# Strassen's algorithm for both products of the MLP, with the first half begun in the out product

## The chip, the cores and the metric

One Trainium2 chip, one core. The metric is the device time of one launch in microseconds, as the median of the runs. Times of single operations come from one profiled execution.

The engines of a core run their own instruction streams in order and wait for one another by semaphores: TensorE (PE in the profile) multiplies, with weight loads (PEld) of their own; VectorE (DVE), ScalarE (ACT) and GpSimd (POOL) do the rest; SyncE (SP) issues the DMA transfers.

## The reference

One decoder layer over 1024 tokens of 1024 features: an attention branch and a time-mixing branch (RWKV-7), their gated merge and out product, and then the MLP, which most of the change concerns:

```python
mix_out = merged @ w_out[l]
x = (x + gt1 * rms_norm(mix_out, norm_mix_post[l])).astype(x.dtype)

h = rms_norm(x, norm_ffn_pre[l]) * (1.0 + sc2) + sh2
f = jnp.square(jax.nn.relu(h @ w_ff1[l])) @ w_ff2[l]      # 1024 -> 4096 -> 1024
x = (x + gt2 * rms_norm(f, norm_ffn_post[l])).astype(x.dtype)
```

The time mixing is computed for pairs of heads and in 16 chunks of tokens: for each head and chunk a Gram product, 64 features of the head deep, is formed first.

## The kernel before

The stages follow one another: attention (to about 500 us), time mixing (to about 1300), merge (to about 1480), out product (to about 1576), MLP (to the end).

**Exact products.** Every large product is computed in three fp32r matmuls: each operand is split into a high part and a remainder, and hi*hi, hi*lo and lo*hi are summed. `split` (L62 to L66) makes them: ScalarE casts the high part (L65), and VectorE or, where it is named, GpSimd subtracts it from the whole (L66). A matmul has 128 contracted rows, 128 columns of weights and 512 moving columns.

**MLP.** The 4096 hidden features are 32 tiles of 128. `ff1` makes two tiles at a time: 8 contracted blocks x 3 products x 2 halves of the tokens, 48 matmuls of L308 per tile, 1536 in all; ScalarE squares the ReLU, and the tile is split at once and stays in SBUF. `ff2` adds the product of the two feature tiles with their rows of `w_ff2` to the result of all 8 token tiles (1536 matmuls of L1162; VectorE adds each PSUM tile to the sum, L1168). Weights come as 128 KB loads `w_t` (L293, two staging tiles) and 512 KB loads `w2t` (L1126) on SyncE's queue; their splits run on ScalarE and VectorE. GpSimd only scales in the last block (L1139).

**Out product and the join.** `out_product` goes over token tiles: product (L984), norm and residual, then `transposed` turns the normed tile into feature rows (TensorE L1043), scales them on VectorE (L1052, L1053) and ScalarE (L1048) and splits them into `hh`, `hl`. Before the tokens 512 to 1023 are through, `ff1_head` starts the first two feature tiles with the first half of the tokens (L308).

**Gram products.** `pair_gram` (L734) has for each of 4 blocks and each of 2 heads one PSUM tile of 4 products (L750), which VectorE then masks into two tiles (L754, L756). The two heads' features lie in partitions 0 to 63 and 64 to 127. `attend` (L494) forms the attention's scores, also 64 deep, head by head in turn (L503).

**Order.** A scheduler orders each engine's stream when the program is built, by the code's order and by when tiles come free; tiles of one name share a ring of buffers, so that a new tile waits for the last use of an old one.

Of the kernel before, what the change touches and what calls it, by code (L numbers as in the profile page):

```python
# [29 lines left out]
NP2 = 6  # L30
NPS = 0
# [19 lines left out]
class Block:  # L51
# [682 lines left out]
    def pair_gram(self, st, pr, m):  # L734
# [229 lines left out]
    def out_product(self, cst, big, w1, psD, psS, xS):  # L964
# [3 lines left out]
        with ExitStack() as es:  # L968
# [66 lines left out]
            def transposed(group, xs):  # L1035

                hh, hl = hhs[group[0] // 4], hls[group[0] // 4]
                for n, i in enumerate(group):
                    x, tl = xs[n], slice(128 * (i % 4), 128 * (i % 4) + 128)
                    for b in range(2):  # L1040
# [4 lines left out]
                        ht = t2.tile([128, 4, 128], F32, name="ht")  # L1045
# [11 lines left out]
            for group in OGR:  # L1057
                todo.append((group, residual(group)))
                if len(todo) > 1:
                    transposed(*todo.pop(0))  # L1060
            self.hh2, self.hl2 = [[[t[:, k, :] for k in range(KT)] for t in ts_] for ts_ in (hhs, hls)]
            self.ff1_head(w1, psD)
            transposed(*todo[0])

    def load_w1(self, w1, j):
        return self.load_w(w1, self.w("w_ff1")[:, 128 * j:128 * j + 128], "w", 2, 8, 2)

    def ff1_head(self, w1, psD):
# [27 lines left out]
    def mlp(self, cst, big, w1, psD, psS, xS):  # L1096
        nc, tc = self.nc, self.tc
        FB = 2
        with ExitStack() as es:
            pool = lambda n, b, **kw: self.pool(es, n, b, **kw)  # L1100
            yp, w2, fp, sm = pool("yp", 1), pool("w2", 2 * FB), pool("fp", 2 * FB), pool("sm3", 4)
            g2 = yp.tile([128, D], F32, name="g2")
            nc.sync.dma_start(g2, self.row_bc(self.rS[1][0]))
            yb = [big.tile([128, 4, D], F32, name="big") for i in range(2)]
            y = [yb[i // 4][:, i % 4, :] for i in range(NT)]
            nb = DFF // 128 // FB

# [131 lines left out]
```

## Time and profile before

| | us |
|---|---|
| time before, median of 3 runs (2299.31 to 2305.64) | 2300.22 |
| the profiled execution, its own time | 2297.36 |
| its span | 2295.6 |
| TensorE busy | 2151.7 |
| VectorE busy | 1365.4 |
| ScalarE busy | 943.3 |
| GpSimd busy | 392.9 |
| last matmul of the MLP ends | 2285.07 |

The rows of the trace are in a section of their own below. A window row gives a stretch, its length, and the busy time of each engine in it (with the number of instructions), then the granted TensorE clock as a share of full speed. A row of the chain of waits gives the start, the duration and the engine, tile and line of one piece of the chain that ended last. A timeline row joins instructions of a group that follow one another and, in brackets, the idle time before them. Two matmul records belong to one fp32 product, as L503 and L750 are, and one to an fp32r product, as L308, L984 and L1162 are; some records can be missing.

### The profile page before, as it was taken

To read this page: it belongs to the slowest core of one execution; us is meant where nothing else is said; L and a number is where in the kernel's file an instruction comes from. 1 tells how busy PE (TensorE), PEld (TensorE's weight loads), DVE (VectorE), ACT (ScalarE), POOL (GpSimd) and SP (SyncE) were. 2 spreads that over 40 slices of the span, in tenths; PEclk is the share of its full clock that TensorE was granted. 3 is DMA by queue.
4 is the path that set the end of the run, shared out by engine and by line. 5 is a ranking of instruction groups with operands and counts; after the bars stand their busy time and mean duration, and the time that the engine had idled before them with its cause. 6 is when DMAs were issued, how large, how long until landed. Compare 5 with 4: busy or idle time off the path is not lost. (4 is left out here: it accounts for less than half of the span.)

```text
span 2295.6 us, 28645 instructions
## 1 busy us (share of the span) xinstructions
PE 2151.7 (94%) x10410; PEld 1705.6 (74%) x10410; DVE 1365.4 (59%) x2638; ACT 943.3 (41%) x1868; POOL 392.9 (17%) x388
## 2 busy tenths in 40 slices
PE   6898999988998989898999999998999999999998
PEld 3676676766776767777777778876888888888887
DVE  5845555467979788777978634338434434434435
ACT  5544534345455546445554442227422222232222
POOL 2504310321313222221313123201000000000002
PEclk9899999998999999989998999999999999999999
DMA  7513311100111010101011264413221111111113
GB/s 252 171 31 102 101 35 38 54 26 21 31 31 36 29 36 24 47 19 42 27 33 49 69 203 148 142 51 114 82 60 40 49 58 42 46 58 44 37 42 147
DMA packets 151212, 152.96 MB, mean 67 GB/s; under 512 B 10618, under 2 KB 118292, under 8 KB 151072
## 3 DMA queue, kind: packets, MB, share of 16 engines
q1 hardware_dynamic: 151071, 151.14, 20.7%
q8 instruction: 82, 1.34, 0.2%
q14 instruction: 59, 0.48, 0.1%
HBM read 129.07 MB, written 22.03 MB: 66 GB/s over the span
## 5 line engine op out<-in xcount | busy, mean ns | idle before, releaser
L65 ACT CAST w_h<-w_t 128x256 fp32r<-128x256 f32 x368 | 147.8, 404 | 480.2 <-PE d L308 366.6
L308 PE MATMUL d<-hh,w_h 128*128 128x512 f32 x960 | 327.7, 413 | 8.2 <-ACT w_h L65 4.7
L308 PE MATMUL d<-hl,w_h 128*128 128x512 f32 x960 | 331.9, 416 | 2.9 <-DVE hl L281 2.9
L308 PE MATMUL d<-hh,w_l 128*128 128x512 f32 x960 | 324.5, 410 | 0.1
L308 PE MATMUL d<-big,w_h 128*128 128x512 f32 (+1 forms) x1056 | 281.1, 385 | 1.9 <-ACT big L65 1.4
L66 POOL TENSOR_TENSOR w_l<-w_t,w_h 128x256 fp32r<-128x256 f32 x160 | 128.3, 803 | 634.9 <-ACT w_h L65 288.4
L308 PEld LDWEIGHTS d<-big,w_h 128*128 128x128 f32 x1056 | 197.9, 190 | 41.5 <-ACT big L65 1.8
L308 PEld LDWEIGHTS d<-hh,w_h 128*128 128x128 f32 x960 | 181.1, 193 | 46.7 <-ACT w_h L65 5.5
L1168 DVE TENSOR_TENSOR big<-big,d 128x1024 f32<-128x1024 f32 (+1 forms) x113 | 136.8, 1211 | 132.3 <-PE d L1162 132.2
L308 PEld LDWEIGHTS d<-hl,w_h 128*128 128x128 f32 x960 | 180.9, 192 | 45.0 <-issue 9.8
L308 PEld LDWEIGHTS d<-hh,w_l 128*128 128x128 f32 x960 | 181.0, 192 | 42.3 <-issue 8.6
L66 DVE TENSOR_TENSOR w_l<-w_t,w_h 128x256 fp32r<-128x256 f32 x208 | 102.0, 492 | 168.0 <-ACT w_h L65 102.1
L308 PE MATMUL d<-big,w_l 128*128 128x512 f32 (+1 forms) x528 | 163.9, 384 | 0.0
L1162 PE MATMUL d<-w2l,fh 128*128 128x512 f32 x512 | 158.3, 389 | 0.0
L1162 PE MATMUL d<-w2h,fl 128*128 128x512 f32 x512 | 158.3, 389 | 0.0
L1162 PE MATMUL d<-w2h,fh 128*128 128x512 f32 x512 | 158.3, 389 | 0.0
L65 ACT CAST w2h<-w2t 128x1024 fp32r<-128x1024 f32 x32 | 33.7, 1052 | 270.2 <-PE d L1162 238.7
L1139 POOL TENSOR_TENSOR big<-big,g 128x1024 f32<-128x1024 f32 x6 | 14.4, 2396 | 670.8 <-DVE big L1168 670.8
L154 POOL TENSOR_TENSOR macc<-macc,ada_t 128x512 f32<-128x512 f32 x56 | 87.8, 1571 | 177.6 <-ACT macc L152 158.9
L308 PEld LDWEIGHTS d<-big,w_l 128*128 128x128 f32 x528 | 100.1, 190 | 19.3
L1162 PEld LDWEIGHTS d<-w2h,fl 128*128 128x128 f32 x512 | 96.1, 188 | 20.0
L1162 PEld LDWEIGHTS d<-w2h,fh 128*128 128x128 f32 x512 | 96.1, 188 | 19.9
(337 smaller groups left out, 3788.1 us busy)
## 6 DMA issues: line engine op xcount, KB each, us to landing
w_t<-in_w_in_dram SPq DMA_DIRECT2D x240, 128.0 KB
ada_t<-in_ada_w_dram SPq DMA_DIRECT2D x64, 256.0 KB
w_t<-in_w_ff_dram SPq DMA_DIRECT2D x128, 128.0 KB
w2t<-in_w_ff_dram SPq DMA_DIRECT2D x32, 512.0 KB
x<-in_x_dram SPq DMA_DIRECT2D x16, 512.0 KB
ada_t<-in_ada_w_dram SPq DMA_DIRECT2D x16, 512.0 KB
gS<-gt SPq DMA_DIRECT2D x32, 256.0 KB
wbr_t<-in_w_branch_dram SPq DMA_DIRECT2D x16, 320.0 KB
```

Of the source, the lines that this page charges most:

```text
L65: nc.scalar.copy(hi, t)
L66: (eng or nc.vector).tensor_tensor(lo, t, hi.bitcast(F32), OP.subtract)
L154: nc.gpsimd.tensor_tensor(acc, acc, t, OP.add)
L308: nc.tensor.matmul(p[:, 512 * half + cs.start:512 * half + cs.stop], a, b[half][k][:, cs], start=k == ks[0] and i == 0, stop=k == ks[-1] a ...
L1139: (nc.vector if i >= NP2 else nc.gpsimd).tensor_tensor(z[i][:, cs], y[i][:, cs], g2[:, cs], OP.mult)
L1162: nc.tensor.matmul(p[:, cs], a[:, ts_], w[:, cs], start=e == 0 and n == 0, stop=e == len(r) - 1 and n == 2)
L1168: nc.vector.tensor_tensor(y[i][:, cs], y[i][:, cs], p[:, cs], OP.add)
```

## The change

**Strassen.** A product of 2 x 2 blocks takes 7 block products in place of 8 in the form of Winograd. Both MLP products use it, each as a phase of its own, so that the features go to DRAM (`fS`) between them.

- `ff1`: 16 pairs of feature tiles (256 features). Blocks of features x contracted halves x token halves; a block product is 12 matmuls, a pair 84 in place of 96. The operands on the tokens' side (T1 to T4, B22) are made once, those on the weights' side (S1 to S4) per pair, all split by ScalarE and VectorE.
- `ff1_head`: for the first 8 pairs the products P1 and P2, which need only the first half of the tokens, run in the out product, 24 matmuls per pair, two pairs ahead of the last transposition and six behind it. P1 goes to DRAM (`uS`); P1 + P2 is the first feature block.
- `ff2`: 8 chunks of 512 features. Seven go by Strassen: 168 matmuls in place of 192; a block product is 24 matmuls into 2 x 2 PSUM banks, and VectorE gathers it into five sums (11, U, 22, 21, 12) of 4 x 512 columns a partition. Splits and sums of the features run on VectorE (`va`), those of the weights on GpSimd (`vb`). The last chunk is plain, by token rows, each followed by norm and output.
- `transposed` for tokens 512 to 1023 keeps the rows whole (`h1`) and makes T2 = B22 - (B12 - B11).
- `pair_gram` takes both heads' PSUM tiles at once and goes over products before heads.

The diff, cut to its core:

```diff
@@ pair_gram
         for b in range(4):
-            for h in range(2):
-                hp = slice(64 * h, 64 * h + 64)
-                p = psS.tile([128, 4, 128], F32, name="s")
-                for c in range(4):
-                    cc = 4 * b + c
-                    nc.tensor.matmul(p[:, c, :].rearrange("p (a t) -> p a t", t=32),
+            ps = [psS.tile([128, 4, 128], F32, name="s") for h in range(2)]
+            for c in range(4):
+                cc = 4 * b + c
+                for h in range(2):
+                    hp = slice(64 * h, 64 * h + 64)
+                    nc.tensor.matmul(ps[h][:, c, :].rearrange("p (a t) -> p a t", t=32),
                                      bk[hp, cc].rearrange("p a t -> p (a t)"), ar4[hp, :, cc, :],
                                      start=True, stop=True)
+            for h in range(2):
+                p = ps[h]
@@ out_product, transposed
-                        self.split(ht, hh[:, 4 * b:4 * b + 4, tl], hl[:, 4 * b:4 * b + 4, tl])
+                        if i < 4:
+                            self.split(ht, self.hh0[:, 4 * b:4 * b + 4, tl], self.hl0[:, 4 * b:4 * b + 4, tl])
+                    if i >= 4:
+                        t = t2.tile([128, 4, 128], F32, name="ht")
+                        nc.vector.tensor_tensor(t, self.h1[:, 0:4, tl], self.hh0[:, 0:4, tl].bitcast(F32), OP.subtract)
+                        nc.vector.tensor_tensor(t, t, self.hl0[:, 0:4, tl].bitcast(F32), OP.subtract)
+                        nc.vector.tensor_tensor(t, self.h1[:, 4:8, tl], t, OP.subtract)
+                        self.split(t, self.T2[:, 0, :, tl], self.T2[:, 1, :, tl])
...
-            self.ff1_head(w1, psD)
+            self.ff1_head(w1, ut, ft, psD, range(2))
             transposed(*todo[0])
+            self.ff1_head(w1, ut, ft, psD, range(2, NH))
+    def ff1_head(self, w1, ut, ft, psD, gs):
...
+            for n, (g, p) in enumerate(pair):
+                self.quarter(p, ws[0][n], hs(range(4)), True)
+                u = ut.tile([128, 512], F32, name="u")
+                self.nc.scalar.copy(u, p)
+                self.nc.sync.dma_start(self.uS[g], u)
+            for n, (g, p) in enumerate(pair):
+                self.quarter(p, ws[1][n], hs(range(4, 8)), False)
+                self.feature(ft, p, 2 * g, 0)
+    def feature(self, ft, p, j, half):
+        t = ft.tile([128, 512], F32, name="ft")
+        nc.scalar.activation(t, p, AF.Relu)
+        nc.scalar.activation(t, t, AF.Square)
+        nc.sync.dma_start(self.fS[j // 4][:, j % 4, 512 * half:512 * half + 512], t)
+    def quarter(self, p, a, b, start):
+        for k, ((ah, al), (bh, bl)) in enumerate(zip(a, b)):
+            for i, (s, m) in enumerate(((ah, bh), (ah, bl), (al, bh))):
+                self.nc.tensor.matmul(p, s, m, start=start and k == 0 and i == 0, stop=k == len(a) - 1 and i == 2,
+                                      skip_group_check=not start)
+    def ff1(self, big, big2, opn, tmp, ut, ft, ps):
...
+        with self.tc.high_priority():
+            for q in range(2):
...
+                nc.vector.tensor_tensor(t, h1[:, k2], h1[:, ks], OP.subtract)
+                self.split(t, T3[:, 0, ks], T3[:, 1, ks])
...
+        def weights(g):
+            raw = tmp.tile([128, KT, 256], F32, name="t8")
+            nc.sync.dma_start(raw, src[:, :, 256 * g:256 * g + 256])
...
+            sums = tmp.tile([128, 4, 4, 128], F32, name="t8")
...
+            nc.vector.tensor_tensor(S1, A[2, 1], A[2, 2], OP.add)
...
+                o = opn.tile([128, 2, 4, 128], F32R, name="op")
+                self.split(t, o[:, 0], o[:, 1])
...
+            run("P6", x[:, 1], True)
+            nc.vector.tensor_tensor(u, u, x[:, 1], OP.add)
...
+            run("P7", y[:, 0], True)
+            v = ut.tile([128, 512], F32, name="u")
+            nc.vector.tensor_tensor(v, u, y[:, 0], OP.add)
+            run("P5", y[:, 1], True)
+            nc.vector.tensor_tensor(v, v, y[:, 1], OP.add)
+            self.feature(ft, v, 2 * g + 1, 1)
...
+    def ff2(self, big, big2, opn, tmp, ut, sm, ps, xS):
...
+            (va, vb), f = (nc.vector, nc.gpsimd), {}
+            ops = {"P1": (operand(fr[:, k1, h1], va), operand(wr[:, k1, h1], vb))}
+            va.tensor_tensor(sa[:, 0], fr[:, k1, h2], fr[:, k2, h2], OP.add)
+            va.tensor_tensor(sa[:, 1], sa[:, 0], fr[:, k1, h1], OP.subtract)
+            vb.tensor_tensor(sb[:, 0], wr[:, k1, h2], wr[:, k1, h1], OP.subtract)
+            vb.tensor_tensor(sb[:, 1], wr[:, k2, h2], sb[:, 0], OP.subtract)
...
+                        nc.vector.tensor_tensor(acc[nm][h], acc[nm][h], ps2[h], OP.add)
...
+            product("P1", x, True)
+            gather("U", x, True)
+            ops["P6"] = operand(sa[:, 1], va), operand(sb[:, 1], vb)
```

The pools of the MLP are `opn` with 12 operand tiles of 4 KB a partition, `tmp` with two tiles of each name (`t8`, `t4`), and PSUM as four tiles of two banks (`m`).

TensorE in the first pair of heads, at the first Gram group: `s` is the PSUM tile of a head and a block, `ar` and `b8` the operands. Before:

```order
L750 MATMUL s_4023<-ar_3972,b8_3973 128x128 x4
L750 MATMUL s_4030<-ar_3972,b8_3973 128x128 x4
L308 MATMUL d_4226<-hh_437,w_l_4217 128x512 x2
L308 MATMUL d_4226<-hh_437,w_h_4222 128x512 x2
L308 MATMUL d_4226<-hl_438,w_h_4222 128x512 x2
L308 MATMUL d_4226<-hh_437,w_l_4223 128x512 x2
L308 MATMUL d_4226<-hh_437,w_h_4222 128x512 x2
L308 MATMUL d_4226<-hl_438,w_h_4222 128x512 x2
L308 MATMUL d_4226<-hh_437,w_l_4223 128x512 x2
L308 MATMUL d_4302<-hh_437,w_h_4280 128x512
L750 MATMUL s_4037<-ar_3972,b8_3973 128x128 x4
L750 MATMUL s_4044<-ar_3972,b8_3973 128x128 x4
```

After:

```order
L749 MATMUL s_4039<-ar_3988,b8_3989 128x128
L749 MATMUL s_4040<-ar_3988,b8_3989 128x128
L749 MATMUL s_4039<-ar_3988,b8_3989 128x128
L749 MATMUL s_4040<-ar_3988,b8_3989 128x128
L749 MATMUL s_4039<-ar_3988,b8_3989 128x128
L749 MATMUL s_4040<-ar_3988,b8_3989 128x128
L749 MATMUL s_4039<-ar_3988,b8_3989 128x128
L749 MATMUL s_4040<-ar_3988,b8_3989 128x128
L307 MATMUL d_4242<-hh_453,w_l_4233 128x512 x2
```

Eight products in two runs of four have become eight in turn; this is the first of the pair's four groups. At the second group the row after is x3, x3, x1, x1, at the third and fourth x4, x4 as before.

VectorE at the join, from the last token tiles on: `ht` is a transposed tile, `w_l` the remainder of a weight tile. Before:

```order
L1052 TENSOR_TENSOR ht<-s,m_574 128x512
L1053 TENSOR_TENSOR ht<-ht,m_574 128x512
L66 TENSOR_TENSOR w2l<-w2t,w2h 128x1024
L66 TENSOR_TENSOR big<-ht,big 128x4x128 x2
L66 TENSOR_TENSOR w_l<-w_t,w_h 128x256 x2
L66 TENSOR_TENSOR w2l<-w2t,w2h 128x1024
L66 TENSOR_TENSOR w_l<-w_t,w_h 128x256
L66 TENSOR_TENSOR fl<-ft,fh 128x1024
L66 TENSOR_TENSOR w_l<-w_t,w_h 128x256
L66 TENSOR_TENSOR fl<-ft,fh 128x1024
L66 TENSOR_TENSOR w_l<-w_t,w_h 128x256
```

After, where `t` and `big` of 128x1024 are the tokens' operands:

```order
L1061 TENSOR_TENSOR ht<-big,ht 128x512
L65 TENSOR_TENSOR big<-ht,big 128x4x128
L65 TENSOR_TENSOR w_l<-w_t,w_h 128x256
L1147 TENSOR_TENSOR t_13418<-big 128x1024
L1147 TENSOR_TENSOR t_13422<-big 128x1024
L65 TENSOR_TENSOR w_l<-w_t,w_h 128x256
L65 TENSOR_TENSOR big<-t_13418,big 128x1024
L65 TENSOR_TENSOR big<-big 128x1024
L65 TENSOR_TENSOR big<-t_13422,big 128x1024
L1152 TENSOR_TENSOR t_13426<-big 128x1024
L1152 TENSOR_TENSOR t_13436<-big 128x1024
L1153 TENSOR_TENSOR t_13426<-t_13426,big 128x1024
```

Ten more rows of `big` and `t` follow before the next `w_l`; 16 instructions of 128x1024 stand between these two weight splits.

VectorE in the steady state of ff2, one block before (`fl`, `w2l`: remainders of features and weights; `big<-big,d`: the sum from PSUM):

```order
L1168 TENSOR_TENSOR big<-big,d 128x1024
L66 TENSOR_TENSOR fl<-ft,fh 128x1024
L1168 TENSOR_TENSOR big<-big,d 128x1024 x6
L66 TENSOR_TENSOR w2l<-w2t,w2h 128x1024
L1168 TENSOR_TENSOR big<-big,d 128x1024
L66 TENSOR_TENSOR w_l<-w_t,w_h 128x256
L66 TENSOR_TENSOR w2l<-w2t,w2h 128x1024
L66 TENSOR_TENSOR w_l<-w_t,w_h 128x256 x3
L66 TENSOR_TENSOR fl<-ft,fh 128x1024
L66 TENSOR_TENSOR w_l<-w_t,w_h 128x256 x4
```

and part of a chunk after (`op`: an operand's remainder; `big<-big,m`: the sums from PSUM; `t`: sums of operands):

```order
L65 TENSOR_TENSOR op<-big,op 128x1024
L1282 TENSOR_TENSOR big<-big,m 128x1024
L1264 TENSOR_TENSOR t_15945<-big 128x1024
L1265 TENSOR_TENSOR t_15945<-t_15945,big 128x1024
L1282 TENSOR_TENSOR big<-big,m 128x1024
L65 TENSOR_TENSOR op<-t_15681,op 128x1024
L1282 TENSOR_TENSOR big<-big,m 128x1024 x2
L65 TENSOR_TENSOR op<-big,op 128x1024
L1282 TENSOR_TENSOR big<-big,m 128x1024 x2
L65 TENSOR_TENSOR op<-t_15945,op 128x1024
L1295 TENSOR_TENSOR t_15945<-big,t_15945 128x1024
L1282 TENSOR_TENSOR big<-big,m 128x1024 x2
```

GpSimd has no instruction there before; after, one chunk is:

```order
L1266 TENSOR_TENSOR t_16474<-big 128x1024
L1267 TENSOR_TENSOR t_16474<-big,t_16474 128x1024
L65 TENSOR_TENSOR op<-big,op 128x1024
L65 TENSOR_TENSOR op<-t_16474,op 128x1024
L1296 TENSOR_TENSOR t_16474<-big,t_16474 128x1024
L65 TENSOR_TENSOR op<-big,op 128x1024
L65 TENSOR_TENSOR op<-t_16588,op 128x1024
L1299 TENSOR_TENSOR t_16852<-big 128x1024
L65 TENSOR_TENSOR op<-t_16474,op 128x1024 x2
L65 TENSOR_TENSOR op<-big,op 128x1024
```

VectorE's splits stand each between two pairs of sums from PSUM, and GpSimd's eleven instructions are new.

## Rows read from the trace of the kernel before

**Rows 1.** The page: busy time by engine, granted clock in 40 slices, chain by line.
```profile
PE 2151.7 (94%) x10410; PEld 1705.6 (74%) x10410; DVE 1365.4 (59%) x2638; ACT 943.3 (41%) x1868; POOL 392.9 (17%) x388
...
PEclk9899999998999999989998999999999999999999
...
PE d L1162 15%; PE d L308 15%; DVE big L66 0%; DVE junk L1024 0%; DVE x L1026 0%; ACT junk L1029 0%; DVE ht L1052 0%; ACT x L1032 0%; ACT junk L1015 0%; PE s L1043 0%; ACT ht L1048 0%; DVE big L1147 0%; DVE my L1013 0%; DVE ht L1053 0%; DVE rn_t L1092 0%
```

**Rows 2.** Chain of waits, 1700 to 1800: start us, us, what.
```profile
1700.24 21.76 PE d L308 x96
1722.00 21.76 PE d L1162 x96
```

**Rows 3.** Windows by stage: stretch, its us, busy us of each engine, clock, DMA.
```profile
core 0: us, PE busy (x) PEld busy (x) DVE busy (x) ACT busy (x) POOL busy (x), PEclk, DMA share, GB/s
500.00:600.00 100.00, 90.13 (x489) 72.19 (x488) 83.17 (x187) 49.51 (x104) 19.16 (x25) 0.93 0.08 22
1590.00:1600.00 10.00, 6.50 (x54) 6.12 (x52) 6.94 (x20) 7.04 (x20) 1.57 (x1) 0.97 0.57 191
1600.00:1610.00 10.00, 7.17 (x31) 6.50 (x32) 5.79 (x9) 6.61 (x12) 0.00 (x0) 0.51 0.27 86
1700.00:1800.00 100.00, 100.00 (x443) 82.81 (x442) 40.64 (x47) 26.37 (x39) 0.00 (x0) 1.00 0.19 57
```

**Rows 4.** Chain of waits, 1570 to 1606 and beyond: the join.
```profile
1577.27 5.08 PE d L308 x21
...
1601.23 1.10 PE s L1043 x4
1602.36 0.70 DVE ht L1052
...
1603.69 1.22 DVE w2l L66
1604.91 0.61 DVE big L66
1605.57 29.39 PE d L308 x142
```

**Rows 5.** Chain of waits, 2230 to the end.
```profile
2285.07 0.69 DVE big L1168
...
2286.79 1.29 DVE big L1147
...
2291.65 0.66 DVEq L1235
```

**Rows 6.** Timeline of TensorE, a Gram group: start, us, line, out<-in, records.
```profile
484.42 1.71 PE L750 MATMUL s<-ar,b 64*128 64x128 f32 x16 [2.49 <-DVE ar L710]
486.06 0.73 PE L308 MATMUL d<-hh,w_l 128*128 128x512 f32 x2
```

**Rows 7.** Timeline of TensorE in the attention, scores of one and of two heads.
```profile
128.04 0.70 PE L503 MATMUL s<-k,q 64*128 64x256 f32 x2
128.67 0.44 PE L522 MATMUL s<-ident,pr 128*128 128x128 f32 x2
...
129.40 0.70 PE L503 MATMUL s<-k,q 64*128 64x256 f32 x4
130.03 1.09 PE L534 MATMUL po<-pts,vt 128*64 128x128 f32 x14
```

**Rows 8.** Timeline of VectorE in the merge.
```profile
1380.80 1.22 DVE L942 SCALAR_TENSOR_TENSOR gr<-gr,d 128x1024 f32<-128x1024 f32 x1 [5.67 <-PE d L308]
1381.94 0.82 DVE L66 TENSOR_TENSOR wbr_l<-wbr_t,wbr_h 128x640 fp32r<-128x640 f32 x1
...
1387.91 2.47 DVE L66 TENSOR_TENSOR wbr_l<-wbr_t,wbr_h 128x640 fp32r<-128x640 f32 x1 [0.47 <-ACT wbr_h L65]
```

**Rows 9.** Timeline of SyncE's queue after the join.
```profile
1604.94 0.33 SPq L1126 DMA_DIRECT2D w2t<-in_w_ff_dram  x1
...
1626.56 15.19 SPq L293 DMA_DIRECT2D w_t<-in_w_ff_dram  x9
```

**Rows 10.** Groups by line on VectorE, 1600 to the end: busy, mean ns, idle before.
```profile
L1168 DVE TENSOR_TENSOR big<-big,d 128x512 f32<-128x512 f32 x2 | 1.4, 685 | 0.1
```

**Rows 11.** Groups by line on GpSimd, 1640 to the end.
```profile
L1139 POOL TENSOR_TENSOR big<-big,g 128x1024 f32<-128x1024 f32 x6 | 14.4, 2396 | 670.8 <-DVE big L1168 670.8
```

**Rows 12.** Timeline of GpSimd in the merge.
```profile
1386.84 2.86 POOL L66 TENSOR_TENSOR big<-wos,big 128x1024 fp32r<-128x1024 f32 x1 [1.68 <-ACT big L65]
1394.98 2.40 POOL L66 TENSOR_TENSOR big<-wos,big 128x1024 fp32r<-128x1024 f32 x1 [5.28 <-ACT big L65]
```

**Rows 13.** Timeline of VectorE in the time mixing.
```profile
691.25 0.41 DVE L756 TENSOR_TENSOR fe<-s,gmask 128x256 f32<-128x256 f32 x1
691.58 0.42 DVE L754 TENSOR_TENSOR b<-s,gmask 128x256 f32<-128x256 f32 x1
691.91 0.41 DVE L756 TENSOR_TENSOR fe<-s,gmask 128x256 f32<-128x256 f32 x1
```

**Rows 14.** Timeline of GpSimd in the time mixing.
```profile
691.31 1.29 POOL L728 TENSOR_TENSOR rkv<-rkv 128x512 f32<-128x512 f32 x1
```

**Rows 15.** Waits of SyncE's queue, 1600 to 1900: sum, times, longest.
```profile
SPq L1126 <- DMA w2t<-in_w_ff_dram: 11.1, 8, 4.4
```

More of the change, by code (lines that the diff above doesn't have):

```diff
@@ L29 @@
 DFF = 4096
-NP2 = 6
-NPS = 0
+NH, NU, NF, NOP = 8, 4, 3, 12
 OGR = ((0, 1), (2, 3), (4,), (5,), (6,), (7,))
@@ L1044, in transposed @@
                                                 self.ident)
-                        ht = t2.tile([128, 4, 128], F32, name="ht")
+                        ht = t2.tile([128, 4, 128], F32, name="ht") if i < 4 else self.h1[:, 4 * b:4 * b + 4, tl]
                         if b:
@@ L1053, in transposed @@
                             nc.vector.tensor_tensor(ht, ht, bc(sh), OP.add)
-                        self.split(ht, hh[:, 4 * b:4 * b + 4, tl], hl[:, 4 * b:4 * b + 4, tl])
+                        if i < 4:
[6 more added lines that the diff above has]
+                        self.split(t, self.T2[:, 0, :, tl], self.T2[:, 1, :, tl])
             todo = []
             for group in OGR:
+                if group[0] == 0:
+                    self.hh0, self.hl0 = [big.tile([128, KT, 512], F32R, name="big") for q in range(2)]
+                if group[0] == 4:
+                    self.h1 = big.tile([128, KT, 512], F32, name="big")
+                    self.T2 = big.tile([128, 2, 4, 512], F32R, name="big")
                 todo.append((group, residual(group)))
@@ new lines, in ff1_head @@
+    def ff1_head(self, w1, ut, ft, psD, gs):
+        hs = lambda ks: [(self.hh0[:, k, :], self.hl0[:, k, :]) for k in ks]
+        for g0 in gs[::2]:
+            d = psD.tile([128, S], F32, name="d")
+            pair = [(g, d[:, 512 * (g - g0):512 * (g - g0) + 512]) for g in (g0, g0 + 1)]
+            w = lambda g, k: self.load_w(w1, self.w("w_ff1")[512 * k:512 * k + 512, 256 * g:256 * g + 128], "w", 2, 8, 2)
+            ws = [[w(g, k) for g, p in pair] for k in range(2)]
+            for n, (g, p) in enumerate(pair):
[6 more added lines that the diff above has]
+                self.feature(ft, p, 2 * g, 0)
@@ L1195, in build @@
             cst = pool("cst", 1)
-            psD, dr = pool("psD", 2, space=PSUM), pool("dr", 1, space=DRAM)
+            dr = pool("dr", 1, space=DRAM)
             oS = [dr.tile([128, S], F32, name=f"oS{j}") for j in range(10)]
@@ L1199, in build @@
             self.rS = [dr.tile([1, D], F32, name=f"rS{j}") for j in range(2)]
+            self.fS = [dr.tile([128, 4, S], F32, name=f"fS{j}") for j in range(8)]
+            self.uS = [dr.tile([128, 512], F32, name=f"uS{j}") for j in range(NH)]
             xS = [dr.tile([128, D], F32, name=f"xS{j}") for j in range(8)]
+            ep = es.enter_context(ExitStack())
+            psD = self.pool(ep, "psD", 2, space=PSUM)
             with tc.tile_pool(name="hp", bufs=1, reuse_waits="tile") as hp, tc.tile_pool(name="wp", bufs=2, reuse_waits="tile") as wp:
@@ L1212, in build @@
                 self.merge(big, psD, oS, gS)
-                psS = pool("psS", 2, space=PSUM)
+                psS = self.pool(ep, "psS", 2, space=PSUM)
+                ut, ft = pool("ut", NU, side="right"), pool("ft", NF, side="right")
                 with tc.tile_pool(name="w1", bufs=2, reuse_waits="tile") as w1:
-                    self.out_product(cst, big, w1, psD, psS, xS)
-                    self.mlp(cst, big, w1, psD, psS, xS)
+                    self.out_product(cst, big, w1, ut, ft, psD, psS, xS)
+                ep.close()
+                big2, tmp, sm, opn = [pool(n, b, side="right") for n, b in (("big2", 2), ("tmp", 2), ("sm3", 4), ("opn", NOP))]
+                ps = pool("psM", 4, space=PSUM)
+                self.ff1(big, big2, opn, tmp, ut, ft, ps)
+                self.ff2(big, big2, opn, tmp, ut, sm, ps, xS)
 _INS = ['x', 'c', 'positions', 'ada_w', 'ada_b', 'norm_mix_pre', 'norm_mix_post', 'norm_ffn_pre', 'norm_ffn_post',
```

269 lines of the change are left out of this document (169 added, 100 removed).

## The prediction

> **What bounds the kernel now.** I read the page first, for the engine that is full: TensorE is busy 94% of the span, VectorE 59%, GpSimd 17%, and of the third of the span that the chain covers, 30% of the span is TensorE's, 15% for each of lines 308 and 1162 [rows 1]. Then the chain of waits in the MLP: it is nothing but blocks of 96 matmuls of 21.76 us each, ff1 (L308) and ff2 (L1162) in turn [rows 2]. One 128x512 matmul there costs 21.76 / 96 = 0.2267 us. The windows by stage say the same: from 1700 on TensorE is 100.00% busy at a granted clock of 1.00, the 2.4 GHz level, while VectorE is 40% busy and GpSimd not at all [rows 3]. So in the MLP a matmul less is 0.2267 us less, as long as nothing else becomes late. The place where TensorE is not full is the join of out product and MLP: it is busy 6.50 of 10 us in 1590 to 1600 and 7.17 of 10 in 1600 to 1610, the latter at a clock of 0.51 (the 1.2 GHz level), and the chain leaves it there for VectorE and ScalarE until 1605.57 [rows 3, 4]. The MLP has 3072 matmuls, 696.4 us; from the first ff1 piece of the chain (1577.27) to the last matmul (2285.07) there are 707.8 us [rows 4, 5], so 11.4 us are lost, all at that join. The last 10.5 us of the span, from 2285.07 to 2295.6, are the end of the last row [rows 5].
>
> The profiled execution took 2297.36 us, 2.9 us under the median of 2300.22. I sum against 2297.4 and add 2.9.
>
> **TensorE's work, -81.6 us.** ff1 goes from 1536 matmuls to 16 pairs x 84 = 1344, ff2 from 1536 to 7 chunks x 168 + 192 = 1368: 360 fewer, x 0.2267 = 81.6 us. This is the whole gain; the other terms say how much of it stays.
>
> **Gram, -4 us (0 to -10).** Eight products, four of one head and then four of the other, run now in 1.64 us (484.42 to 486.06), 16 records of 0.103 us, one after the other [rows 6]. What alternation of two heads on different halves of the rows is worth shows in the attention's scores: one matmul alone (2 records) takes 0.63 us to the next instruction, the two heads' matmuls together (4 records) also 0.63 [rows 7]. But the order shows that the change mostly doesn't alternate: of four groups per pair only the first does, since the second pair of tiles comes free one after the other; in the rest the rows read x4, x4 as before. Neighbours of different heads rise from 25 to 70. I take one record, 0.103 us, for each: 45 x 0.103 = 4.6, of which some stand between other products: -4; two records each gives -10.
>
> **Head of the MLP, +16 us (+3 to +20).** The head is 192 matmuls, 43.5 us. In front of its end VectorE has new work. For each of four token tiles three more subtractions and one split fewer, 2 x 0.6 (the piece at 1604.91 [rows 4]), 4 x 1.2 = 5 us before the last transposition is through: 1605 becomes 1610. Then the operands T3, T1, T4 and B22, at high priority: 12 sums and 8 splits of 128x1024, 16 of them between two weight splits in VectorE's order. Their start-to-start time is 1.14 us (1380.80 to 1381.94 [rows 8]), so 18.3 us, to 1628. Behind them stand 11 splits of head weights; two are staged, and 9 loads wait: SyncE issues a w_t load when one of two staging tiles is free, in before nine in 15.19 us, 1.69 us each [rows 9]: 1628 + 15.2 = 1643. (SyncE's queue holds the stores of u and of the features between these loads, each behind the ScalarE operation that writes them; that is in the upper bound.) The last quarter (12 x 0.2267) and the first operand of ff1 make it 1648. Without stalls the head would end at 1577.3 + 43.5 = 1620.8. So 27 us are lost where 11.4 are lost now: +16. If loads and splits catch up it is +3, the 5 us of subtractions less some slack; with a clock of 0.51 for another 10 us, +20.
>
> **ff1, +9 us (+2 to +28).** A pair of the first eight is 60 matmuls, 13.6 us, a later one 84, 19.0 us. VectorE has 8 to 10 us per pair (128x512 split or sum 0.69, start to start 0.60), ScalarE about as much, GpSimd nothing. What is tight is the PSUM half that is read and written again three times a pair with four or five matmuls between, 0.9 to 1.1 us. The addition takes 0.69 [rows 10]; alone it is hidden, behind one split it is 1.3 and 0.4 late. With VectorE two-thirds busy I take half a us per pair: 16 x 0.55 = 9. SyncE issues 5 to 6 transfers per pair at 0.34 us [rows 9], and the load of the next weights stands behind feature stores; a pair in which that is late pays it whole. Nothing but the opening is +2. All three late in each pair, 16 x 3 x 0.4 = 19, with 9 for loads, is +28.
>
> **From ff1 to ff2, +4 us (+1 to +12).** wr(0) is loaded after the last pair's P7, the feature block before; the chain is a 512 KB load, a sum of 2.40 us and a split of 2.40 us on GpSimd [rows 11], and P1 (5.4 us) covers most of it.
>
> **ff2, +25 us (+6 to +118).** A chunk is 168 matmuls, 38.1 us. GpSimd gets what it never had in this stage: per chunk 7 splits and 4 sums of 128x1024, 11 x 2.396 = 26.4 us [rows 11]. VectorE has 7 splits, 4 sums and 14 additions from PSUM, 25 x 1.14 = 28.5 us; alone, both fit in 38.1. They don't run side by side. In the merge a VectorE split (0.82 alone) took 2.47 us and a GpSimd split (2.40 alone) took 2.86, where they met [rows 8, 12]: they went one after the other. A VectorE operation with one input in PSUM is not held: products of 0.41 to 0.42 us keep their time inside a GpSimd operation of 1.29, which isn't stretched either [rows 13, 14]. So 11 VectorE operations of 1.14 and 11 of GpSimd exclude each other: 12.5 + 26.4 = 38.9 us, already over TensorE's 38.1, and that is the best a chunk can do: 7 x 0.8 = +6. It needs VectorE's additions to lie under GpSimd's operations each time. At worst each of VectorE's 11 waits for a whole GpSimd operation: 28.5 + 11 x 2.40 = 54.9, 7 x 16.8 = +118. An operation that comes at any moment waits half of one: 28.5 + 11 x 1.2 = 41.7, 7 x 3.6 = +25; I take that, since the split of 2.47 us had waited 1.65 of a possible 2.4 and not every one meets a GpSimd operation. There is room for three products in the 12 operand tiles, so lateness isn't absorbed for long. A clock under 1.00 would not add: at 91% busy it was granted 0.93 [rows 3], and 38.1 / 0.93 = 41.0 is still under 41.7.
>
> The Trainium skill ("SBUF — State Buffer", "Who interferes with whom") says that a VectorE instruction with two SBUF inputs and a GpSimd instruction that reads SBUF lock each other out for the whole instruction, whoever starts first, and that one with a single SBUF input isn't held. By that rule a chunk takes at least the time of both together, so TensorE isn't the bound of ff2 after the change; the rows agree in both parts, and the terms above are theirs.
>
> **Last chunk and end, -1 us (-3 to +4).** 192 plain matmuls in rows of 24, 5.4 us, with VectorE at about 5 us per row. After the last matmul there is only one half to add, square and scale, where now the other half's multiplication and output still stand in front (2286.79, 1.29 us [rows 5]): 2 less, with 1 for a late row.
>
> **Sum:** -81.6 - 4 + 16 + 9 + 4 + 25 - 1 = -32.6. 2297.4 - 32.6 = 2264.8; with the 2.9, 2268.
>
> **Rivals.**
> *TensorE stays the bound everywhere.* Weight splits overtake, loads come early, additions lie under GpSimd's work: -81.6 - 4 + 5 + 3 + 2 + 6 - 3 = -72.6, 2228. For it: VectorE's and GpSimd's sums are each under a chunk. Against it: 38.9 against 38.1, and the order puts splits directly behind additions that wait for TensorE. 0.22.
> *GpSimd and VectorE take turns in ff2 badly, and the kernel is slower.* Each operand is late, TensorE waits, its results come later, and so do the additions in front of the next split in VectorE's order. The price is 7 us for each us of a chunk; the other terms leave 57.6 us, so it decides from 38.1 + 57.6 / 7 = 46.3 us per chunk, and at 54.9 gives 2361. For it: both rows of the merge are lengthened at the first meeting. Against it: 14 of VectorE's 25 are free of it. 0.16.
> *ff1's weights bound it.* 1 MB per pair goes through two tiles that hold raw weights and sums in turn. Two 512 KB loads of 4.4 us (the longest that SyncE's queue waited for one [rows 15]) and some 11 operations of 0.6 in series are 15.4 us against 13.6 in the first eight pairs: +14, 2282. Against it: VectorE's sums can start before TensorE needs them. 0.14.
> *The Gram products don't alternate* is part of the forecast: 4 us, no sign changes with it.
>
> **How the numbers follow.** Forecast 0.48, the rivals 0.22, 0.16 and 0.14. About 0.3%, 7 us, is what a measurement of this kernel can tell from no change. The first rival is faster, the forecast too but for 0.03, the third but for 0.01, and of the second 0.03 lies within 7 us: faster 0.80, same 0.07, slower 0.13. Range: down to a little under the first rival, 2222; up to where half of the second is left out, a chunk of 48 us, 2312.
>
> **What would show it.** In the chain of ff2 pieces of VectorE L65 and GpSimd between TensorE's; VectorE splits of 128x1024 with a mean over 1.5 us, GpSimd's over 2.6, and PSUM additions still at 1.22; chunks of some 42 us. In the head, TensorE waiting for w_l near 1625 to 1645. Gram groups of 0.9 us where they alternate. It is wrong if chunks stay at 38, if the head ends near 1625, or if TensorE waits for loads in ff1.

## The result and the profile after

The changed kernel takes 2280.56 us (median of 5 runs, 2272.03 to 2282.83), the kernel before 2300.22: a ratio of 0.990 (95% interval 0.988 to 0.992). That is 19.7 us faster, and 12.6 us slower than the forecast of 2268. In a second series it was 0.988 (0.985 to 0.991). The profiled execution has a span of 2279.2 us, against 2295.6.

The page of the changed kernel, the lines that answer to [rows 1]:

```profile
PE 2090.6 (92%) x10002; PEld 1628.6 (71%) x10002; DVE 1567.8 (69%) x2845; ACT 1036.3 (45%) x2018; POOL 621.9 (27%) x461
...
PE 12%; DVE 8%; POOL 7%; issue 3%; DMA 1%; ACT 1%; DVEq 0%; POOLq 0%; SPq 0%; ACTq 0%
```

TensorE is busy 61 us less, VectorE and GpSimd some 200 each more, and the chain is no longer TensorE's alone. Where its time stands now is shown by the windows, which answer to [rows 3]:

```profile
core 0: us, PE busy (x) PEld busy (x) DVE busy (x) ACT busy (x) POOL busy (x), PEclk, DMA share, GB/s
1620.00:1640.00 20.00, 4.61 (x14) 2.58 (x12) 20.00 (x20) 7.04 (x10) 0.00 (x0) 0.73 0.16 51
1640.00:1660.00 20.00, 17.11 (x60) 12.73 (x60) 6.33 (x14) 7.79 (x17) 0.00 (x0) 0.85 0.42 131
1800.00:1820.00 20.00, 20.00 (x86) 15.62 (x85) 10.45 (x17) 9.52 (x17) 0.00 (x0) 1.00 0.31 106
2040.00:2060.00 20.00, 20.00 (x90) 16.57 (x89) 18.79 (x16) 7.04 (x7) 15.35 (x6) 1.00 0.55 210
2220.00:2240.00 20.00, 14.96 (x58) 11.69 (x57) 15.52 (x23) 3.76 (x12) 2.58 (x1) 0.83 0.00 0
```

ff1 (1800) is full as the MLP was before. In 1620 to 1640 TensorE has 4.61 us of work and VectorE 20.00; in 1640 to 1660 the clock is 0.85. In ff2 (2040) VectorE has 18.8 and GpSimd 15.4 of 20 us beside a full TensorE, and in the last chunk (2220) TensorE has a gap. The stages' borders are in its timeline: first matmul of the head, last of the head and first of ff1, first of ff2, first of the last chunk, the gap in it, last of all:

```profile
1581.53 0.48 PE L1108 MATMUL d<-big,w_h 128*128 128x512 f32 x1
...
1659.71 0.39 PE L1108 MATMUL d<-big,w_l 128*128 128x512 f32 x1
1661.29 6.12 PE L1108 MATMUL m<-big,op 128*128 128x512 f32 x24 [1.19 <-ACT op L64]
...
1940.04 0.40 PE L1108 MATMUL m<-op 128*128 128x512 f32 x1
...
2217.76 3.19 PE L1108 MATMUL m<-op 128*128 128x512 f32 x13
2225.99 18.32 PE L1108 MATMUL m<-op 128*128 128x512 f32 x71 [5.04 <-DVE op L65]
...
2268.08 3.04 PE L1108 MATMUL m<-op,t 128*128 128x512 f32 x12 [1.27 <-DVE ss L1117]
```

Head 79.8 us (1581.53 to 1661.29) for 43.5 of matmuls; ff1 278.8 for 261.2; seven chunks 277.7 (1940.04 to 2217.76, 1176 matmuls) for 266.6; last chunk 53.4, with the gap of 5.04 behind its first 13 matmuls, for 43.5; end 8.1 where it was 10.5. Sum of the differences: -81.6 for the 360 matmuls; head +36.3 less the 11.4 lost before, +24.9; ff1 +17.6; chunks +11.1; last chunk and end +7.4; and the head starts 4.3 us later than the chain's first piece of before (1577.27 [rows 4]). Together -16.3, and the spans differ by 16.4. (The very first head matmul of before starts at 1576.47; counted from there the start is 5.1 later and the head +24.1.)

What TensorE waited for, sum, times and longest:

```profile
PE d L1108 <- DVE w_l L65: 13.5, 1, 13.5
PE d L1108 <- ACT u L1090: 9.0, 7, 2.7
PE m L1108 <- POOL op L65: 6.4, 9, 1.8
PE m L1108 <- DVE op L65: 5.2, 2, 5.0
```

### The profile page after: what moved, and what is told of

Its sections match the earlier page's. It is cut to its first block, busy times and chain, and to the rows that moved or that the text cites. A ratio compares the mean times of both kernels' runs of the same rounds, so it can differ in the third digit from the quotient of the medians.

```text
span 2279.2 us, 28241 instructions
## 1 busy us (share of the span) xinstructions
PE 2090.6 (92%) x10002; PEld 1628.6 (71%) x10002; DVE 1567.8 (69%) x2845; ACT 1036.3 (45%) x2018; POOL 621.9 (27%) x461
## 5 line engine op out<-in xcount | busy, mean ns | idle before, releaser
L1108 PE MATMUL m<-op 128*128 128x512 f32 x1272 | 295.8, 394 | 11.5 <-POOL op L65 6.4
L1108 PEld LDWEIGHTS m<-op 128*128 128x128 f32 x1272 | 240.0, 190 | 66.9 <-POOL op L65 10.6
L1108 PE MATMUL m<-big,op 128*128 128x512 f32 x1152 | 275.1, 399 | 5.1 <-ACT op L64 2.1
L1108 PEld LDWEIGHTS m<-big,op 128*128 128x128 f32 x1152 | 212.8, 188 | 67.3 <-DVE u L1220 4.2
L307 PEld LDWEIGHTS d<-hh,w_h 128*128 128x128 f32 x960 | 180.8, 193 | 46.3 <-issue 5.7
L64 ACT CAST op<-t 128x512 fp32r<-128x512 f32 (+1 forms) x152 | 114.2, 776 | 182.8 <-PE m L1108 121.5
L65 DVE TENSOR_TENSOR op<-t,op 128x512 fp32r<-128x512 f32 (+1 forms) x124 | 118.5, 975 | 28.0 <-ACT op L64 27.8
L1282 DVE TENSOR_TENSOR big<-big,m 128x1024 f32<-128x1024 f32 x88 | 104.4, 1210 | 3.8 <-PE m L1108 3.8
L775 DVE TENSOR_TENSOR lt<-lt 64x30 f32<-64x30 f32 (+14 forms) x240 | 96.9, 404 | 8.2
L777 DVE TENSOR_TENSOR lt<-lt 64x30 f32<-64x30 f32 (+14 forms) x240 | 94.2, 392 | 7.7
L874 PEld LDWEIGHTS ch<-sv,fe 128*128 128x128 f32 x512 | 83.3, 191 | 20.3 <-DVE sv L877 8.9
L65 POOL TENSOR_TENSOR op<-t,op 128x1024 fp32r<-128x1024 f32 x28 | 93.2, 3339 | 4.3 <-ACT op L64 4.3
```

The costliest lines, as they stand in the source:

```text
L64: nc.scalar.copy(hi, t)
L65: (eng or nc.vector).tensor_tensor(lo, t, hi.bitcast(F32), OP.subtract)
L307: nc.tensor.matmul(p[:, 512 * half + cs.start:512 * half + cs.stop], a, b[half][k][:, cs], start=k == ks[0] and i == 0, stop=k == ks[-1] a ...
L775: nc.vector.tensor_tensor(q, lb[:, s + 1:32, s:s + 1].to_broadcast([64, n, s]), lb[:, s:s + 1, 0:s].to_broadcast([64, n, s]), OP.mult)
L777: nc.vector.tensor_tensor(lb[:, s + 1:32, 0:s], lb[:, s + 1:32, 0:s], q, OP.add)
L874: nc.tensor.matmul(ps[h][:, c8, :], fe[b][:, h, c8, :], sv[h][b][:, c8, :], start=True, stop=True)
```

## Experiments

All times are medians; the ratio is to the kernel before on the same chip. The kernels whose names begin with np or h4, and hp_last, contain the edit of noprio.

### The changed kernel again

> The changed kernel once more, on the chip that times the other kernels of this series, so that they have a common base. Expected: a ratio of 0.990 to the kernel before, as in the first timing (2280.6 against 2300.2 us), and chunks of 38.7 us in ff2.

2274.06 us, ratio 0.988 (0.985 to 0.991). Its profiled execution has a span of 2266.9 us, 12 less than the first one of the same program, and two places make most of that up. One is the second pair of heads, where the first execution had a lower clock. Windows of the first execution, then of this one (stretch, its us, busy us, clock, DMA):

```profile
580.00:590.00 10.00, 10.00 (x51) 8.20 (x49) 7.48 (x21) 1.56 (x3) 1.81 (x2) 0.83 0.04 13
590.00:600.00 10.00, 10.00 (x49) 8.09 (x48) 7.56 (x21) 3.62 (x5) 2.91 (x4) 0.74 0.06 16
```

```profile
580.00:590.00 10.00, 10.00 (x60) 8.06 (x59) 8.28 (x24) 3.17 (x6) 4.73 (x5) 1.00 0.09 26
590.00:600.00 10.00, 9.35 (x66) 7.50 (x66) 9.36 (x26) 4.95 (x15) 2.63 (x2) 1.00 0.06 16
```

TensorE was busy for all of the 20 us in the first execution, at 0.83 and 0.74, and in this one nearly, at 1.00: the first loses some 4 us there. The head starts at 1573.24 here, 8.3 us earlier. The other place is ff2: from the third chunk on GpSimd's first sum of a chunk starts every 38.7 us in the first execution (rows further below) and every 38.08 here, the time of 168 matmuls:

```profile
2042.44 2.42 POOL L1266 TENSOR_TENSOR t<-big 128x1024 f32<-128x1024 f32 x1 [1.16 <-DVE op L65]
...
2080.52 2.42 POOL L1266 TENSOR_TENSOR t<-big 128x1024 f32<-128x1024 f32 x1 [1.16 <-DVE op L65]
```

### The Gram products alone

```diff
 # oldgram: the changed kernel with the loop of before; newgram: before with
+            ps = [psS.tile([128, 4, 128], F32, name="s") for h in range(2)]
+            for c in range(4):
+                for h in range(2):
```

> The changed kernel with the Gram products of before (four of one head, then four of the other). The prediction gave the alternation 4 us (0 to 10), for 45 more neighbours of different heads at 0.1 us each: then this kernel is 4 us slower than the changed one. Rival: the profile of the changed kernel needs 1.6 us more from the first Gram product to the out product than before, so the alternation brings nothing where it stands between other products and makes VectorE wait for the second tile; then this kernel is 0 to 2 us faster. In the trace: a fully alternating group of 8 products takes 0.9 us by the first theory and 1.64 by the second.

> The kernel before with nothing but the alternating Gram products. First theory: 4 us under the kernel before (ratio 0.998). Rival: the same to 2 us over it (1.000 to 1.001).

newgram: 2298.11 us, 0.998 (0.996 to 1.000). oldgram: 2280.39, 0.991 (0.988 to 0.993), beside 0.988 (0.985 to 0.991) for the changed kernel. Both lean towards a gain of 3 to 6 us, and the intervals of oldgram and the changed kernel overlap. The first group of the first pair of heads runs at the lower clock in both traces. Four and four in oldgram, with the instruction after it, then alternating in newgram, each with its window:

```profile
486.96 3.09 PE L749 MATMUL s<-ar,b 64*128 64x128 f32 x16 [2.50 <-DVE ar L709]
489.98 1.22 PE L307 MATMUL d<-hh,w_l 128*128 128x512 f32 x2
486.96:489.98 3.02, 3.02 (x16) 2.80 (x17) 2.94 (x5) 0.00 (x0) 1.71 (x1) 0.50 0.00 0
```

```profile
491.60 2.08 PE L750 MATMUL s<-ar,b 64*128 64x128 f32 x16 [2.50 <-DVE ar L710]
493.60 1.22 PE L308 MATMUL d<-hh,w_l 128*128 128x512 f32 x2
491.60:493.60 2.00, 2.00 (x16) 1.78 (x16) 1.93 (x4) 0.00 (x0) 1.71 (x1) 0.50 0.00 0
```

At the same granted clock of 0.50 (the 1.2 GHz level) the eight products take 3.02 us one head after the other and 2.00 alternating: the products of two heads do overlap. Half of 2.00 is 1.0 us at the full clock, an estimate, where [rows 6] had 1.64 in sequence. In the changed kernel the clock falls within this group, and it takes 1.28 us at a mean clock of 0.83 in the first execution and 1.67 at 0.62 in the second. So the step in the prediction holds for a group that alternates. What it is worth in the whole doesn't show in the traces: from the first product with `dgs` (the gate) of pair one to the first of pair eight it is 718.8 us before, 718.2 in newgram, 719.1 and 718.8 in the two executions of the changed kernel, and 724.0 in oldgram, at a clock of 0.93 against 0.94. The clock moves by as much from one execution to the next, and oldgram's profiled chunks of ff2 also had the 38.7 us of the slower pattern. How much of the 3 to 6 us is the alternation's stays open.

### The tokens' operands at their own priority

```diff
-        with self.tc.high_priority():
-            for q in range(2):
...
+        for q in range(2):
...
```

> The changed kernel with the tokens' operands (T3, T1, T4, B22) made at the priority of their place in the code, behind the head's weight splits. Theory: the 13.5 us that TensorE waits for the one weight split behind 16 of these operations come from that order; with the splits first the head ends about 13 us earlier, but P7, P5, P4 and P3 of the first pair then wait for the same 23 us of VectorE, so that 5 to 8 us are left as a gain: 2273 to 2276. Rival: VectorE is full from 1560 to 1640 whatever its order, and only the place of the wait moves: within 3 us of the changed kernel. Third: the operands are late for ff1 and TensorE idles longer than now: 5 to 10 us slower.

2262.45 us, 0.983 (0.980 to 0.985): 11.6 faster than the changed kernel in the same series, more than the 5 to 8 of the first theory and nearly all of its 13. (The two profiled executions are only 3.3 us apart: noprio's head starts 6.4 us later, behind stages that the edit doesn't touch.) The chain of the changed kernel at the head shows what is gone:

```profile
1616.52 1.23 DVE t L1147
...
1618.88 0.34 DVE w_l L65
1619.21 3.41 DVE big L65 x3
...
1635.11 2.27 DVE t L1157 x2
1637.38 0.34 DVE w_l L65
1637.78 2.10 DMA w_t<-in_w_ff_dram
...
1640.86 8.17 PE d L1108 x24
```

From 1619.21, behind a weight split, VectorE works for 18.2 us on 16 operations of 128x1024 before the next split at 1637.38. TensorE's next 24 matmuls in the chain take 8.17 us, where the full clock makes 5.44: the granted clock is 0.50 from 1637.77 to 1646.12, over the first 12 of them. Last matmul of the head and first of ff1, without the priority:

```profile
1641.82 0.39 PE L1108 MATMUL d<-big,w_l 128*128 128x512 f32 x1
1644.87 8.65 PE L1108 MATMUL m<-big,op 128*128 128x512 f32 x24 [2.65 <-ACT op L64]
```

The wait of 13.5 us for w_l is not in the list of waits any more, and the head takes 65.2 us in place of 79.8 to 80.2. ff1 takes 281.0, only 2 to 3 more: the operands were not urgent. The rival that only the place moves falls.

### Head by four pairs

```diff
-        for g0 in gs[::2]:
-            d = psD.tile([128, S], F32, name="d")
+        for g0 in gs[::4]:
+            ds = [psD.tile([128, S], F32, name="d") for g in gg[::2]]
```

> The kernel with the tokens' operands at their own priority, in which the six pairs of the head behind the last transposition go four and two at a time: P1 of four pairs, then P2 of four. Theory: the 8 us that TensorE waits in the head for ScalarE's copies of P1 come from only one product (2.7 us) between the end of P1 and the P2 that writes the same half of a bank; with three between them they go, and the head falls from 65 to 58 us. Rival: the weights' splits on VectorE are what is late there, the wait moves to them, and the time stays within 3 us.

2261.06 us, 0.981 (0.977 to 0.984): the same as noprio. The head takes 63.8 us. The wait for the copies of P1 falls from 8.0 us in noprio to 3.6, and that for the features that ScalarE writes (`ft`) rises from 1.7 to 3.8. The time stays, as the rival said, but the wait moved to the features; the weight splits that the rival named make TensorE wait 0.8 us.

### A third tile for the weights of ff1

```diff
-            raw = tmp.tile([128, KT, 256], F32, name="t8")
+            raw = tmp.tile([128, KT, 256], F32, name="t8", bufs=3)
...
-NH, NU, NF, NOP = 8, 4, 3, 12
+NH, NU, NF, NOP = 8, 4, 3, 11
```

> The kernel with the tokens' operands at their own priority (2262.5 us), with a third tile for ff1's raw weights and weight sums, and 11 operand tiles in place of 12 to make room. Theory: of the 20 us that ff1 takes over its 261 us of matmuls, most is lost in the first five pairs because the load of the next weights waits until the tile of the pair before is free; with three tiles loads run a pair earlier, and ff1 falls from 281 to 270 us or less: 2250 to 2255. Rival: VectorE, which makes the sums and splits of a pair just as late, is the limit there, and the load only seems to be: ff1 stays within 3 us of 281. The tile less for operands may cost ff2 up to 3 us; that is read from its chunks.

2273.59 us, 0.988 (0.983 to 0.992), slower than noprio. All tiles of the name `t8` have the third buffer. ff1 takes 277.3 us against 281.0, near the rival's 3, and 2.3 of the 3.7 are in its first pair, where noprio's TensorE runs at the lower clock. So the load is not the main limit, as far as this run tells with one operand tile less in ff1 too. Nor did the theory start from a right reading: in noprio the first five pairs lose 9.0 of the 19.8 us that ff1 takes over its matmuls, not most. The operand tile less costs more than expected: chunks of ff2 go to 39.7 us (VectorE's first sum of a chunk at 2033.9, 2073.57, 2113.25), and TensorE's waits for GpSimd's operands from 6.7 to 12.1 us. The head takes 69.3 us, 4.1 more than in noprio, with 5.3 us of waiting for ScalarE's weight casts; why isn't shown.

### ff2: what VectorE and GpSimd share

```diff
 # np_sums
-            vb.tensor_tensor(sb[:, 0], wr[:, k1, h2], wr[:, k1, h1], OP.subtract)
+            va.tensor_tensor(sb[:, 0], wr[:, k1, h2], wr[:, k1, h1], OP.subtract)
...
 # h4_alldve
-            (va, vb), f = (nc.vector, nc.gpsimd), {}
+            (va, vb), f = (nc.vector, nc.vector), {}
```

> The kernel with the tokens' operands at their own priority, in which the four sums of the weights per chunk of ff2 run on VectorE and not on GpSimd. It moves 4 x 2.40 us off GpSimd and 4 x 1.14 onto VectorE: 33.1 us of VectorE, 16.8 of GpSimd. By the prediction (each VectorE operation waits half a GpSimd operation, 41.7 us per chunk) this would be 33.1 + 15 x 0.55 = 41, no gain. By the mutual exclusion alone (15 x 1 + 16.8 = 32) chunks are TensorE's 38.08 us in every execution, never 38.74, and the entry into ff2 is some us shorter: 0 to 5 us faster. Rival: VectorE's longer stream makes operands late and chunks go over 39.

> The tokens' operands at their own priority and the head four pairs at a time, with all of ff2's splits and sums on VectorE, none on GpSimd. If VectorE is what a chunk of ff2 is measured by, 36 operations of 1.14 us make 41.0 us per chunk, no split of 128x1024 takes longer than 1.25 us, and the kernel is 7 x 2.9 = 20 us slower, 2281. Rival: the operand tiles or the features' loads hold the chunks, not VectorE; then they stay at 38.1 to 38.7 without GpSimd as well.

np_sums: 2286.21 us, 0.992 (0.989 to 0.995), chunks of 44 us: the rival, VectorE's longer stream, is right, and the exclusion alone, which gave 38.08, falls. h4_alldve, which also has the head of np_head4, one run: 2278.42 us, chunks of 43.7 to 44.5 by VectorE's first sum, with one of 39.8, in place of 38.1 to 38.7. In the groups of VectorE from 1960 to 2200 the splits `op<-t` of h4_alldve have their own length, 1219 ns on the mean, and its sums 1218 to 1220; in np_sums, with GpSimd at work, they are stretched to 1987 and up to 3310.

So GpSimd's share is worth 5 to 6 us per chunk here, though its operations keep VectorE waiting. h4_alldve's 44 is over the 41.0 of 36 operations back to back; VectorE is idle there before its additions, mostly for TensorE, whose granted clock is 0.91 from 2040 to 2200 (1.00 in np_sums up to 2144). So it isn't VectorE's length alone, and what the lower clock has of the 3 us isn't shown.

### The last chunk's operands

np_late moves four additions of U behind the first rows; hp_last adds to np_head4:

```diff
+        with self.tc.high_priority():
+            for k in range(2):
+                ks = slice(2 * k, 2 * k + 2)
+                A[0, k] = operand(fr[:, ks, 0:512], nc.vector)
+                B[k, 0] = operand(wr[:, ks, 0:512], nc.vector)
```

> The kernel with the tokens' operands at their own priority, in which the four additions of U to the sums 21 and 22 come after the first two rows of the last chunk. Theory: TensorE waits 5.05 us before the last chunk because three of these additions (4.6 us) stand in VectorE's stream before the last operand's split; without them the wait is under 1 us and the kernel 4 us faster, 2258. Rival: the split waits for the gathers of the last Strassen chunk, which wait for TensorE; then the wait stays at 4 to 5 us.

> The tokens' operands at their own priority and the head four pairs at a time (2261.1 us), and now the operands of the last chunk's first rows at high priority, so that VectorE makes their two late splits directly behind ScalarE's casts and ahead of the last gathers and additions of U. Theory: TensorE's 5.05 us ahead of the last chunk are VectorE's order there (the cast is done 5 us before the split starts); they fall to 1 us or less: 2257. Rival: the operand tiles only come free when P4 is through, and the splits then wait for GpSimd's, so that 3 us or more stay.

np_late: 2267.03 us, 0.983 (0.979 to 0.988), and the same wait of 5.04 us. The scheduler put the additions (L1335) where they were, so this run doesn't decide on them. VectorE there:

```profile
2206.62 1.21 DVE L1281 TENSOR_TENSOR big<-big,m 128x1024 f32<-128x1024 f32 x1
2207.75 2.25 DVE L1335 TENSOR_TENSOR big<-big 128x1024 f32<-128x1024 f32 x1
2209.92 1.21 DVE L1281 TENSOR_TENSOR big<-big,m 128x1024 f32<-128x1024 f32 x1
2211.05 1.21 DVE L65 TENSOR_TENSOR op<-big,op 128x1024 fp32r<-128x1024 f32 x1
```

The split at 2211.05, on which TensorE waits, stands behind two gathers (L1281) and an addition of 2.25 us; ScalarE's casts had been done at 2206.1. hp_last, with the splits ahead: 2255.46 us, 0.978 (0.976 to 0.981), the lowest ratio here, with an interval that overlaps that of np_head4. Of the wait little is gone; it has moved behind the first 31 matmuls of the last chunk:

```profile
PE m L1109 <- DVE big L1346: 4.0, 1, 4.0
```

4.0 in place of 5.05: three gathers (3.48 us) and four additions of U (6.10) that were put off now stand ahead of the addition after the first product. The theory falls; VectorE is full there, whatever the order. The last chunk takes 52.2 us after 54.6 in np_head4, but the chunks before it have the 38.7 us pattern in this execution. The 5.6 us between the two medians are from different series and not explained.

## Why the prediction was right, and where not

The direction and the range were right, the middle 12.6 us too low. The terms were not as good as the sum. Against the first profiled execution:

| term | forecast | measured |
|---|---|---|
| 360 matmuls | -81.6 | -81.6 |
| ahead of the head (Gram) | -4 | +4.3 |
| head | +16 | +24.9 |
| ff1 | +9 | +17.6 |
| ff1 to ff2 (first two chunks) | +4 | +7.8 |
| ff2 (five steady chunks) | +25 | +3.3 |
| last chunk and end | -1 | +7.4 |
| sum | -32.6 | -16.3 |

The largest loss, ff2, was forecast 22 us too high, the other terms together 38 too low. That so much of this cancelled is luck.

**360 matmuls, -81.6.** The table counts them at the 0.2267 us of before. That size held in ff2, where 168 take 38.08 us; ff1 below was slower.

**Head, +16, measured +24.9, over its +20.** The mechanism was the one named, 16 operations between two weight splits, with 18.2 us for the predicted 18.3. The start was late: 1619.2 and not 1610, since an addition of the norm on GpSimd, held to 4.31 us (1.6 in the four tiles before), stands in the chain before it; TensorE had waited 5.9 us for copies by then. And behind it not nine loads at 1.69 us held the head but one of 2.10, 12 matmuls at half the clock, and copies: from 1637.4 to 1660, 22.7 us where the working had 20. noprio confirms the cause: 14.6 us of the head are that order.

**ff1, +9, measured +17.6.** The shape was right, a loss in every pair, and the size half. The chain in the middle and later part of ff1:

```profile
1744.55 184.26 PE m L1108 x775
```

That is 0.238 us per matmul, not 0.227, without a wait that the chain shows. Counted by matmuls, pairs two to fifteen lose 0.4 to 1.1 us each, 11.7 together, where the term had 0.55; the first loses 3.0 and the last 2.9, with waits for VectorE and ScalarE. In most pairs three matmuls start 0.33 us after the one before, which makes a third of a us; the rest is spread over the pair. The loads are not the cause (np_raw3), and VectorE is busy only 10.45 of 20 us at 1800; what is, stays open.

**From ff1 to ff2, +4, measured 7.8,** within its range: the first chunk takes 45.7 us on TensorE, the second 38.3. TensorE waits 4.6 us for GpSimd's operands, as named, and the clock is 0.80 from 1940 to 1945 and 0.86 to 1950.

**ff2, +25, measured +3.3 in the five chunks behind those,** 38.74 us each, and nothing in the executions with 38.08; both are under the lower end of +6. By the prediction's own sign, "It is wrong if chunks stay at 38", this term failed. Its other signs of the exclusion came: long splits on both engines, additions from PSUM as before. VectorE's groups from 1960 to 2200 (count, busy us and mean ns, idle before):

```profile
L1282 DVE TENSOR_TENSOR big<-big,m 128x1024 f32<-128x1024 f32 x80 | 94.7, 1210 | 2.1 <-PE m L1108 2.0
L65 DVE TENSOR_TENSOR op<-t,op 128x1024 fp32r<-128x1024 f32 x25 | 47.1, 1884 | 2.2 <-ACT op L64 2.2
...
L1298 DVE TENSOR_TENSOR t<-big 128x1024 f32<-128x1024 f32 x6 | 19.9, 3315 | 0.2
```

The additions from PSUM keep 1210 ns, as the rows of the time mixing had it [rows 13], and sums take up to 3.3 us. Side by side, VectorE and then GpSimd (which also shows the chunk's beat, 2054.32 to 2093.05):

```profile
2061.24 3.31 DVE L1295 TENSOR_TENSOR t<-big,t 128x1024 f32<-128x1024 f32 x1
2064.47 2.34 DVE L1282 TENSOR_TENSOR big<-big,m 128x1024 f32<-128x1024 f32 x2
```

```profile
2054.32 2.40 POOL L1266 TENSOR_TENSOR t<-big 128x1024 f32<-128x1024 f32 x1 [3.43 <-DVE op L65]
...
2060.03 3.43 POOL L65 TENSOR_TENSOR op<-big,op 128x1024 fp32r<-128x1024 f32 x1
2063.43 3.40 POOL L65 TENSOR_TENSOR op<-t,op 128x1024 fp32r<-128x1024 f32 x1
...
2093.05 2.40 POOL L1266 TENSOR_TENSOR t<-big 128x1024 f32<-128x1024 f32 x1 [3.43 <-DVE op L65]
```

A sum of 3.31 is 2.2 of waiting and 1.1 of work; GpSimd's 3.4 is 2.4 and one operation of VectorE's. The Trainium skill ("SBUF — State Buffer", "Who interferes with whom") has this rule, for whole instructions, and the trace agrees in both parts. The size failed in one number: I let every operation wait for half a GpSimd operation, 1.2 us. All 68 split and sum operations of the window together are 58 us longer than 1.22 each, 0.85 on the mean, since some meet none. 28.5 + 11 x 0.85 = 37.9, with 1.2 of waiting for GpSimd's operand some 39, against 38.74 measured. The lower end, 38.9, was no floor either: 38.08 occurs (again, noprio, np_head4), TensorE's own time. A GpSimd operation is held for 0.9 to 1.0 by one of VectorE, so a chunk's two shares make 26.4 + 11 x 0.95 = 36.9, an estimate. A chunk therefore stands just at the edge between both engines and TensorE. (The row behind the clock of 0.93 has TensorE busy 90% and not 91%; in the steady chunks of both executions it was granted 1.00.)

**Last chunk and end, -1, measured +7.4, over its +4.** The end is 2.4 shorter, as forecast. The last chunk loses 9.8: I left VectorE's additions of U and its last gathers at nothing, and TensorE waits 5.04 us for the operand behind them and then runs at a clock of 0.83 (2220 to 2240).

**Gram, -4.** The step was right where the heads alternate: 2.00 us against 3.02 at the same clock. The order told rightly that most groups don't. In the time it can't be told from how executions differ: against before, the MLP's head starts 4.3 us later in one and 4.0 earlier in the other.

Of the rivals the first, TensorE as the bound everywhere, holds, in some executions, for ff2's steady chunks; the second, slower, stayed far from its point of 46.3 us per chunk, but np_sums with 44 shows how near a small shift of work comes. The third, ff1's weights as the bound with 15.4 us for each of the first eight pairs, falls: a pair's weights come in one load of 5.3 to 5.8 us in the chain, and pairs two to eight take 14.0 to 14.7.

## What to carry to other kernels

When work is saved on the full engine, sum what the second engine has to do in each stage before counting the gain: here 62 of 82 us were lost again, the largest part, 25, in the head, where VectorE is full for 20 us on end. Work that is not needed until the next stage should not have priority over what feeds the full engine now: taking it away gave 12 us. GpSimd can help VectorE even where the two exclude each other: here chunks took 38.1 to 38.7 us with it and 44 without; 14 of VectorE's 25 operations read PSUM and keep their time beside it.

## What the hardware showed unexpectedly

The same program ran its ff2 chunks in 38.08 us in one execution and in 38.7 in another, each steadily from the third chunk on, with the same orders: VectorE and GpSimd fall into one of two patterns of taking turns. What decides between them isn't shown. The granted clock fell to 0.74 to 0.83 in windows in which TensorE was 10.00 of 10 us busy, in one execution and not in the other, around 590 us and far ahead of the MLP; this makes about half of the 8 us between the starts of the MLP's head in the two. A short group has to be read with its clock: eight products over 64 rows that alternate between two heads took 1.67 us at a mean clock of 0.62, as long as 1.64 in sequence at 1.00, but at the same clock 2.00 against 3.02.
